# The order of the three products of a split-precision matmul: lower weights first instead of last

## The chip, the cores and the metric

One core of one Trainium2 chip runs the whole program, once per launch. The metric is device time in microseconds (us). The kernel before takes 658.43 us, the median of 3 runs that lie between 657.54 and 659.13.

## The reference, cut to what matters

The reference is a two-layer decoder trunk on 256 tokens of width 1024 in float32: a gated DeltaNet mixer, a squared-ReLU MLP (1024 to 4096 to 1024), a block-sparse attention mixer (with 256 tokens it is plain causal attention with a linear bias), a second MLP, and a final RMSNorm. What matters here are its dense products with weights:

```
proj = hn @ w_in                                  # DeltaNet: q, k, v, z
o.reshape(b, t, DN_DIM) @ w_out
jnp.square(jax.nn.relu(hn @ w_up)) @ w_down       # twice, once per layer
proj = hn @ w_in                                  # attention: q, k, v
o.transpose(0, 2, 1, 3).reshape(b, t, MB_DIM) @ w_out
```

The result must be close to float32 products, so the kernel splits both operands of each product into an upper part (rounded to the fast float32r format) and a lower part (what the rounding left over).

## The kernel before, in words

**Weights.** All weights come in one stream of 200 tiles ("units") of 128 x 1024 float32, 512 KB each. `prep` (lines 105 to 117) handles one: SyncE starts the DMA into `wf` (3 buffers), ScalarE casts it to the upper part `wh` (line 115, 5 buffers), and VectorE subtracts that from `wf` to get the lower part `wl` (line 116, 5 buffers). The first 8 units are handled in two halves of 512 columns. So of a tile `wh` is always there before `wl`. `unit` (line 121) hands out the next tile and first asks for the four after it (`LEAD = 4`), so that a tile's cast has to wait until TensorE has done with the tile five before it.

**Products.** `mm3` (lines 128 to 131) adds one weight block of 128 x 128 times one activation block of 128 x 256 into a PSUM accumulator, as three matmuls: upper weights by upper activations (line 129), upper weights by lower activations (line 130), lower weights by upper activations (line 131). The first argument after the output is the stationary operand, which is loaded into TensorE by a load of its own before each matmul (PEld in the profile); the second is streamed. The product of the two lower parts is left out. The first matmul of an accumulation carries `start`, the last one `stop`.

`mm3` is called from three places: `pair` (line 194: two columns of blocks over the 8 blocks of the input width, 48 matmuls from two units; used for q, k, v of both mixers and for the MLPs' first product), `project_out` (line 224: the mixers' output products) and `mlp` (line 267: the first layer's second MLP product, 4 outputs of 8 units each). Per unit this makes 8 calls, 24 matmuls. The products `natural` (lines 207 to 222; z and attention's v) and `mlp_last` (lines 322 to 345; the second layer's second MLP product) write their three matmuls with `mm` (line 133) and stream 512 columns of weights.

**Activations.** `Norm.feed` (line 164) makes upper and lower activations of a residual block: ScalarE the upper `xh` (line 167), VectorE the lower `xl` from it (line 168). `Norm.finish` (line 178) sums squares over partitions with small matmuls (`n_ps`) and spreads the scale with two more (`n_pb`, line 190); these stand between the matmuls of `pair` calls.

**Order.** Each engine executes its instructions in the order in which they stand in its queue. That order is made when the program is built: `ORDER` (line 47) and `ATT` (line 52) give the order in which the heads' steps are written, and the Tile framework's planner then takes, on its own costs, at each point the earliest-written instruction that it holds to be ready; it also sets the semaphore waits between engines. Where an instruction has more waits than it can carry, the rest go into EVENT_SEMAPHORE instructions ahead of it. So steps such as transposes and head matmuls stand between matmuls of one and the same `mm3`. VectorE (DVE) does everything in one queue: the `wl` subtractions, the lower activations, the evacuations of PSUM (line 258 in the MLP, lines 245 and 281 for the residual) and the mixers' elementwise steps.

Of the kernel before, what the change touches and what calls it, by code (L numbers as in the profile page):

```python
# [75 lines left out]
def trunk_kernel(ctx: ExitStack, tc: tile.TileContext, xT, wst, wba, par, con, selc, gfin, out):  # L76
    nc = tc.nc
# [48 lines left out]
        return ring[u]  # L126

    def mm3(o, wh, wl, xh, xl, start, stop):
        nc.tensor.matmul(o, wh, xh, start=start, stop=False, skip_group_check=True)  # L129
        nc.tensor.matmul(o, wh, xl, start=False, stop=False, skip_group_check=True)  # L130
        nc.tensor.matmul(o, wl, xh, start=False, stop=stop, skip_group_check=True)  # L131

    def mm(o, l, r, start=True, stop=True):
        nc.tensor.matmul(o, l, r, start=start, stop=stop, skip_group_check=True)  # L134
# [59 lines left out]
    def pair(nm, name):  # L194

        ps = bank("acc", [P, 2, T], f"ps_{name}")
        for c in range(2):
            wh, wl = unit()
            for k in range(4):
                kt = 4 * c + k  # L200
                for n in range(2):
                    s = slice((k * 2 + n) * P, (k * 2 + n + 1) * P)
                    mm3(ps[:, n, :], wh[:, s], wl[:, s], nm.xh[:, kt, :], nm.xl[:, kt, :],
                        kt == 0 and n == 0, kt == KT - 1)
        return ps
# [18 lines left out]
    def project_out(name, oh, ol, hin, nxt):  # L224

        pss = [bank("out" + "abcd"[i], [P, 2, T], f"ps_{name}_{i}") for i in range(4)]

        def piece(hd, n, w):
            s = slice(n * P, (n + 1) * P)
            mm3(pss[n // 2][:, n % 2, :], w[0][:, s], w[1][:, s], oh[:, hd, :], ol[:, hd, :],  # L230
                hd == 0 and n % 2 == 0, hd == H - 1)

        first = H - NLAST
        for hd in range(first):
            w = unit()
            for n in range(KT):
                piece(hd, n, w)
        w = [unit() for _ in range(first, H)]
        hout = act.tile([P, KT, T], F32, tag="h", name=f"h_{name}")
        for n in range(KT):  # L240
            for k in range(H - first):
                piece(first + k, n, w[k])
            if n % 2:
                i = n // 2
                nc.vector.tensor_add(hout[:, 2 * i:2 * i + 2, :], hin[:, 2 * i:2 * i + 2, :], pss[i])
                nxt.feed(hout, i)
        return hout
# [19 lines left out]
    def mlp(name, nm, hin, nxt):  # L267
        with tc.tile_pool(name=f"hid_{name}", bufs=1) as hp:
            hh, hl = mlp_up(hp, name, nm)
            hout = act.tile([P, KT, T], F32, tag="h", name=f"h_{name}")  # L270
            for i in range(KT // 2):
                ps = bank("acc", [P, 2, T], f"ps_dn_{name}_{i}")
                for c in range(8):
                    wh, wl = unit()
                    for k in range(4):
                        kt = 4 * c + k
                        for n in range(2):
                            s = slice((k * 2 + n) * P, (k * 2 + n + 1) * P)
                            mm3(ps[:, n, :], wh[:, s], wl[:, s], hh[:, kt, :], hl[:, kt, :],
                                kt == 0 and n == 0, kt == NFF - 1)  # L280
                nc.vector.tensor_add(hout[:, 2 * i:2 * i + 2, :], hin[:, 2 * i:2 * i + 2, :], ps)
                nxt.feed(hout, i)
        return hout
# [674 lines left out]
```

## Time and profile before

| | us |
|---|---|
| median of 3 runs | 658.43 |
| the profiled execution's own time | 658.23 |
| its span, first to last instruction | 656.4 |
| TensorE matmul busy | 643.4 (98%) |
| TensorE weight loads busy | 605.2 (92%) |
| VectorE busy | 454.6 (69%) |
| ScalarE busy | 345.6 (53%) |

What lies around the span is 658.23 - 656.4 = 1.8 us. In the profile PE is TensorE's matmuls, PEld its weight loads, DVE VectorE, ACT ScalarE, SP SyncE. A matmul row's duration is longer than the step to the next matmul, since matmuls overlap in the engine; where the pace matters, look at start times. By stage: DeltaNet from 10 to 181 us, the first MLP to 363, attention to 467, the second MLP to the end (its last product, by `mm`, from 560 on).

### The profile page before, as it was taken

What the parts mean: (1) busy time and instruction counts of PE and PEld (TensorE: products, weight loads), DVE (VectorE), ACT (ScalarE), POOL (GpSimd) and SP (SyncE); (2) the same over time, 40 slices, a digit from 0 to 9 for tenths busy, and PEclk for the clock granted to TensorE, in tenths of its full rate; (3) what the DMA queues carried; (4) which work ended last, traced back from release to release, by engine and by line L of the source; (5) the groups of instructions that cost most, each with busy time, mean ns of one, the idle gap of its engine ahead of it and who ended that gap; (6) DMA issues with size and microseconds to landing.
All of it is one profiled execution on the core that took longest, in us unless ns stands there. A gap on an engine that the chain in (4) does not pass through costs nothing.

```text
span 656.4 us, 13349 instructions
## 1 busy us (share of the span) xinstructions
PE 643.4 (98%) x5454; PEld 605.2 (92%) x5454; DVE 454.6 (69%) x841; ACT 345.6 (53%) x570; POOL 4.0 (1%) x10
## 2 busy tenths in 40 slices
PE   8999999999999999999999999999999999999995
PEld 6999878979999999999999999889999999888994
DVE  5899998997897666645554668775976666545443
ACT  7689782553575555534443444543655555434331
POOL 1000000000000000000000000000000000000000
PEclk9999999999999999999999999999999999999998
DMA  8754151342555555565555555555365555556531
GB/s 268 240 171 154 36 192 68 103 126 65 187 168 193 187 176 189 187 193 190 179 182 190 184 169 161 165 157 170 119 224 191 185 178 190 171 188 186 190 129 65
DMA packets 32029, 109.42 MB, mean 167 GB/s; under 512 B 3552, under 2 KB 3936, under 8 KB 31968
## 3 DMA queue, kind: packets, MB, share of 16 engines
q1 hardware_dynamic: 31248, 107.71, 49.9%
q8 instruction: 43, 0.70, 0.4%
q10 hardware_dynamic: 720, 0.86, 0.4%
q14 instruction: 18, 0.15, 0.1%
HBM read 107.51 MB, written 1.05 MB: 165 GB/s over the span
## 4 chain that ended last, share of the span: by engine, by line
PE 86%; DVE 6%; DMA 4%; ACT 3%; issue 1%; DVEq 0%; ACTq 0%
PE ps_last L134 12%; PE ps_up_m L130 9%; PE ps_up_m L131 9%; PE ps_up_m L129 9%; PE ps_dn_m L130 5%; PE ps_dn_m L129 5%; PE ps_dn_m L131 5%; PE ps_vn L134 3%; DMA wf<-in_w 3%; PE ps_z L134 3%; DVE wl L116 2%; PE ps_qk L130 2%; PE ps_qk L131 2%; PE ps_qk L129 2%; PE kk L134 2%; PE ps_last_e L134 1%
## 5 line engine op out<-in xcount | busy, mean ns | idle before, releaser
L116 DVE TENSOR_TENSOR wl<-wf,wh 128x1024 fp32r<-128x1024 f32 (+1 forms) x208 | 244.8, 1182 | 144.9 <-ACT wh L115 144.5
L115 ACT CAST wh<-wf 128x1024 fp32r<-128x1024 f32 (+1 forms) x208 | 210.7, 1017 | 244.3 <-PE ps_up_m L130 65.4
L130 PE MATMUL ps_up_m<-n_l,wh 128*128 128x256 f32 x512 | 143.9, 281 | 0.2 <-DVE n_l L168 0.2
L131 PE MATMUL ps_up_m<-n_h,wl 128*128 128x256 f32 x512 | 144.0, 281 | 0.0
L129 PE MATMUL ps_up_m<-n_h,wh 128*128 128x256 f32 x512 | 143.8, 281 | 0.0
L129 PEld LDWEIGHTS ps_up_m<-n_h,wh 128*128 128x128 f32 x512 | 98.0, 192 | 0.0
L130 PEld LDWEIGHTS ps_up_m<-n_l,wh 128*128 128x128 f32 x512 | 96.2, 188 | 0.3 <-DVE n_l L168 0.3
L131 PEld LDWEIGHTS ps_up_m<-n_h,wl 128*128 128x128 f32 x512 | 96.1, 188 | 0.0
L129 PE MATMUL ps_dn_m<-hh_m,wh 128*128 128x256 f32 x256 | 71.9, 281 | 0.0
L130 PE MATMUL ps_dn_m<-hl_m,wh 128*128 128x256 f32 x256 | 71.9, 281 | 0.0
L131 PE MATMUL ps_dn_m<-hh_m,wl 128*128 128x256 f32 x256 | 71.9, 281 | 0.0
L129 PEld LDWEIGHTS ps_dn_m<-hh_m,wh 128*128 128x128 f32 x256 | 49.2, 192 | 0.0
L130 PEld LDWEIGHTS ps_dn_m<-hl_m,wh 128*128 128x128 f32 x256 | 48.1, 188 | 0.0
L131 PEld LDWEIGHTS ps_dn_m<-hh_m,wl 128*128 128x128 f32 x256 | 48.1, 188 | 0.0
L134 PE MATMUL ps_last<-wh,hl_m 128*128 128x512 f32 (+1 forms) x128 | 46.9, 366 | 0.0
L134 PE MATMUL ps_last<-wl,hh_m 128*128 128x512 f32 (+1 forms) x128 | 46.8, 366 | 0.0
L134 PE MATMUL ps_last<-wh,hh_m 128*128 128x512 f32 (+1 forms) x128 | 46.7, 365 | 0.0
L129 PE MATMUL ps_kq<-n_h,wh 128*128 128x256 f32 x128 | 36.5, 285 | 0.0
L129 PE MATMUL ps_qk<-n_h,wh 128*128 128x256 f32 x128 | 36.3, 283 | 0.0
L131 PE MATMUL ps_kq<-n_h,wl 128*128 128x256 f32 x128 | 36.0, 281 | 0.0
L130 PE MATMUL ps_kq<-n_l,wh 128*128 128x256 f32 x128 | 35.9, 280 | 0.0
L130 PE MATMUL ps_qk<-n_l,wh 128*128 128x256 f32 x128 | 35.7, 279 | 0.0
(278 smaller groups left out, 1254.3 us busy)
## 6 DMA issues: line engine op xcount, KB each, us to landing
wf<-in_w SPq DMA_DIRECT2D x192, 512.0 KB, 3.5
wf<-in_w SPq DMA_DIRECT2D x16, 256.0 KB, 3.9
h<-in_x SPq DMA_DIRECT2D x4, 256.0 KB, 6.5
gf<-in_g SPq DMA_DIRECT2D x1, 512.0 KB, 3.8
out<-hg SPq DMA_DIRECT2D x2, 256.0 KB, 2.1
out<-hg ACTq DMA_DIRECT2D x2, 256.0 KB, 2.5
sel<-in_sel SPq DMA_DIRECT2D x1, 448.0 KB, 4.7
cn<-in_con SPq DMA_DIRECT2D x1, 276.0 KB, 5.1
```

The costliest lines, as they stand in the source:

```text
L115: nc.scalar.copy(wh[:, s], wf[:, s])
L116: nc.vector.tensor_sub(wl[:, s], wf[:, s], wh[:, s].bitcast(F32))
L129: nc.tensor.matmul(o, wh, xh, start=start, stop=False, skip_group_check=True)
L130: nc.tensor.matmul(o, wh, xl, start=False, stop=False, skip_group_check=True)
L131: nc.tensor.matmul(o, wl, xh, start=False, stop=stop, skip_group_check=True)
L134: nc.tensor.matmul(o, l, r, start=start, stop=stop, skip_group_check=True)
```

## The change: which product of the three comes first

Only the order of the three matmuls in `mm3` changes. `start` goes to lower weights by upper activations, `stop` to upper weights by lower activations. `natural`, `mlp_last` and everything else are as they were.

```diff
     def mm3(o, wh, wl, xh, xl, start, stop):
-        nc.tensor.matmul(o, wh, xh, start=start, stop=False, skip_group_check=True)
-        nc.tensor.matmul(o, wh, xl, start=False, stop=False, skip_group_check=True)
-        nc.tensor.matmul(o, wl, xh, start=False, stop=stop, skip_group_check=True)
+        nc.tensor.matmul(o, wl, xh, start=start, stop=False, skip_group_check=True)
+        nc.tensor.matmul(o, wh, xh, start=False, stop=False, skip_group_check=True)
+        nc.tensor.matmul(o, wh, xl, start=False, stop=stop, skip_group_check=True)
```

So after the change line 129 is lower weights by upper activations, line 130 upper by upper, line 131 upper weights by lower activations.

## Rows read from the trace of the kernel before

**Rows 1.** The page: span, busy time by engine, chain of waits by engine.
```profile
span 656.4 us, 13349 instructions
PE 643.4 (98%) x5454; PEld 605.2 (92%) x5454; DVE 454.6 (69%) x841; ACT 345.6 (53%) x570; POOL 4.0 (1%) x10
PE 86%; DVE 6%; DMA 4%; ACT 3%; issue 1%; DVEq 0%; ACTq 0%
```

**Rows 2.** Busy time by stretch: us, each engine's busy us (instructions), clock, DMA.
```profile
10.00:90.00 80.00, 78.39 (x589) 71.72 (x588) 75.96 (x207) 63.96 (x159) 1.05 (x2) 1.00 0.50 166
193.00:368.00 175.00, 175.00 (x1488) 175.00 (x1488) 104.87 (x110) 88.80 (x107) 0.00 (x0) 1.00 0.56 188
```

**Rows 3.** Line 129's matmuls: count, ns min/median/max, first to last start us.
```profile
L129 PE MATMUL ps_dn_m<-hh_m,wh x256: 281/281/281, 272.9 to 363.0; 128*128 128x256 f32 x128
...
L129 PE MATMUL ps_up_m<-n_h,wh x221: 281/281/281, 480.9 to 558.7; 128*128 128x256 f32 x111
...
L129 PE MATMUL ps_qk<-n_h,wh x45: 276/276/276, 378.0 to 392.9; 128*128 128x256 f32 x45
...
L129 PE MATMUL ps_a<-at_oh,wh x54: 276/276/276, 447.9 to 466.0; 128*128 128x256 f32 x54
...
L129 PE MATMUL ps_kq<-n_h,wh x128: 276/276/683, 10.1 to 64.8; 128*128 128x256 f32 x128
...
L129 PE MATMUL ps_g<-gd_oh,wh x64: 276/276/384, 150.8 to 180.6; 128*128 128x256 f32 x64
```

**Rows 4.** Timeline of PE around one break at 192 us: start, duration, operation.
```profile
191.90 0.28 PE L129 MATMUL ps_up_m<-n_h,wh 128*128 128x256 f32 x1
192.01 0.28 PE L130 MATMUL ps_up_m<-n_l,wh 128*128 128x256 f32 x1
192.13 0.60 PE L134 MATMUL n_pb<-cn,n_col 128*128 128x128 f32 x4
192.49 0.36 PE L131 MATMUL ps_up_m<-n_h,wl 128*128 128x256 f32 x1
192.69 0.28 PE L129 MATMUL ps_up_m<-n_h,wh 128*128 128x256 f32 x1
192.81 0.28 PE L130 MATMUL ps_up_m<-n_l,wh 128*128 128x256 f32 x1
```

**Rows 5.** Timeline of the first two weight tiles, 10.8 to 14.2 us.
```profile
10.80 0.69 DVE L116 TENSOR_TENSOR wl<-wf,wh 128x512 fp32r<-128x512 f32 x1 [0.18 <-ACT wh L115]
...
11.44 0.19 PEld L129 LDWEIGHTS ps_kq<-n_h,wh 128*128 128x128 f32 x1
...
11.66 0.19 PEld L131 LDWEIGHTS ps_kq<-n_h,wl 128*128 128x128 f32 x1
...
11.81 1.29 DVE L116 TENSOR_TENSOR wl<-wf,wh 128x512 fp32r<-128x512 f32 x2
...
14.16 0.19 PEld L129 LDWEIGHTS ps_kq<-n_h,wh 128*128 128x128 f32 x1
```

**Rows 6.** Who waited for whom: us in total, times, longest us.
```profile
PE kqt L507 <- DVE kq L500: 1.0, 1, 1.0
...
DVE wl L116 <- ACT wh L115: 144.5, 139, 3.3
ACT wh L115 <- PE ps_up_m L130: 65.4, 55, 2.1
```

**Rows 7.** Timeline of TensorE and DVE at the hand-over to the first MLP.
```profile
182.53 1.22 DVE L116 TENSOR_TENSOR wl<-wf,wh 128x1024 fp32r<-128x1024 f32 x1
...
183.67 0.39 PE L129 MATMUL ps_up_m<-n_h,wh 128*128 128x256 f32 x2
183.67 0.88 DVE L168 SCALAR_TENSOR_TENSOR n_l<-h_g,pm,n_h 128x256 fp32r<-128x256 f32 x2
...
184.21 0.38 PE L130 MATMUL ps_up_m<-n_l,wh 128*128 128x256 f32 x1 [0.15 <-DVE n_l L168]
```

**Rows 8.** Line 129's extra waits on TensorE's queue: count, ns, first and last start.
```profile
L129 PEldq EVENT_SEMAPHORE  x41: 51/51/51, 15.2 to 552.3; - x41
```

## The prediction

> **What bounds the kernel now.** I read the page first: TensorE's matmuls are busy 98% of the span, and the chain of waits that ended last lies to 86% on TensorE [rows 1]. So the question is what sets the pace of the matmul stream and where it is broken. Second the busy time by stretch: from 193 to 368 us matmuls and weight loads are busy 175.00 of 175.00 us while DVE works 104.87; from 10 to 90 us matmuls miss 1.6 of 80 us and DVE is nearly as full, 75.96 of 80 [rows 2]. There alone can a late weight tile matter.
>
> Third the starts of line 129, one per call of `mm3`, which give the pace. In the first MLP's second product 255 steps take 363.0 - 272.9 = 90.1 us: 0.3533 us per call, 117.8 ns per matmul. In the second MLP 220 steps take 77.8 us: 0.3536. But in attention 44 steps take 14.9 us and 53 steps 18.1 us, together 33.0 / 97 = 0.340 us, 113.4 ns per matmul [rows 3]. The same operation of the same shape has two paces, 3.9% apart, and the rows' durations (281 against 276 ns) tell which one a stretch has. A stretch keeps its pace; it changes only where other matmuls break in, as at 192.13, where `n_pb` stands between the upper and the lower product of one call: two starts before it are 0.11 apart, two behind it 0.12 [rows 4], and it then stays slow to 368 us. What chooses the pace I can't tell from the trace; it is the largest unknown.
>
> **The change part by part.** Nothing is added or removed: 24 matmuls and 24 loads per tile stay. Against the profiled execution's 658.23 us (span 656.4 and 1.8 around it), 0.2 below the median of 658.43.
>
> *The stream itself.* Write a call as (weights, activations): before (H,h)(H,l)(L,h), after (L,h)(H,h)(H,l). Calls follow one another without a break, so the stream of before, started one step later, is the stream of after: two uses of one upper tile side by side, then one lower; each load still overlaps the same kind of matmul. Only the step to the next block moves, from behind (L,h) to behind (H,l). A break then resumes at another member of the call. So I cost the pace at 0. Bounds: if both long slow stretches became fast, the first (175.0 us) would give 175.0 x (1 - 0.340/0.3533) = 6.6 us and the second (77.8 us) 3.0: -9.6. If the pieces whose median is 276 (128 + 64 + 45 + 54 = 291 calls in rows 3) became slow: 291 x 0.0133 = +3.9. I take 0, since it is the row with both members next to a break, `n_pb` in the middle of a call [rows 4], that the new order only renames.
>
> [...]
>
> *Lower weights asked for two matmuls earlier.* `wl` is ready after `wh`, and a call now begins with it. In the stream the cast waits for the release of an old tile (55 waits in the MLPs, rows 6), and then four tiles of 24 matmuls pass, 4 x 24 x 0.1178 = 11.3 us, before the new one is used; cast and subtraction need 2.3 of these (the subtraction is 1.22, rows 7). Two matmuls, 0.24 us, come off a margin of 9: nothing. At the start the margin is small. Tile 0's second half: DVE ends `wl` at 10.80 + 0.69 = 11.49, line 131 loads it at 11.66, and its first call begins at 11.44 [rows 5]. The load of 11.44 is now that of `wl`: with about 0.1 us from DVE's end to TensorE's start (the first of the two lower activations begun at 183.67 ends near 184.11, the matmul starts at 184.21, rows 7) it starts at 11.59, 0.15 late. Behind it wait only TensorE's own matmuls. Tile 1's first half ends near 12.46 and is due 12 matmuls after 11.44, at 12.80; its second half at 13.10 against 14.16 [rows 5]. No other is late. The 0.15 us is covered: at 32.85 TensorE waits 1.0 us for DVE's first head step anyway [rows 6], whose chain runs over DMA, ScalarE and DVE. Without that cover +0.15. I take 0.
>
> *Lower activations asked for later.* At 183.67 two upper products run ahead, then TensorE waits until 184.21 for `n_l` [rows 7]: 0.54 us for two matmuls of 0.113, so 0.32 idle. Now each of these two calls has two matmuls that don't need it; four run, to 183.67 + 4 x 0.1134 = 184.12, and 0.23 us of the wait is filled. Bounds 0 (the planner sets them otherwise) and -0.32. What is late next is the same DVE queue, where a `wl` subtraction of 1.22 us stands ahead of `n_l` [rows 7], so I take -0.2.
>
> *Upper weights released later.* `wh` is now read by the last matmul of a tile, one step of 0.118 us later; the cast starts that much later, and DVE, which waits 139 times for a cast [rows 6], holds what is queued behind its subtraction: residual adds, lower activations, evacuations. In the stream nobody waits for these (175.00 of 175.00). At the two output projections' hand-overs they lie ahead of the next matmuls: 0 to 2 x 0.12 = +0.24. At the one seen, the subtraction at 182.53 waits for no cast [rows 7], so 0.
>
> [...]
>
> *Waits on TensorE's queue.* Line 129 has 41 extra waits of 51 ns [rows 8]: it needs ScalarE's `wh` and, through DVE, a free accumulator. Now its weights come from DVE too, and `wh` is the wait of the next matmul, so many of the 41 may go: at most 41 x 0.051 = -2.1 us; as many new ones would be +2.1. Hidden by matmuls in flight in the full stretch [rows 2]: 0.
>
> Sum: 0 + 0 - 0.2 + 0 + 0 = -0.2: 658.0 for the profiled execution, 658.2 for the median.
>
> **The rivals.**
>
> *A: the fast pace is found (faster).* A break that resumes elsewhere leaves the long stretch from 193 us fast: 658.2 - 6.6 = 651.6; the stretch from 481 us alone 655.2; both 648.6. For it: the pace is chosen at a break, and nothing in the operation forbids 113.4 ns. Against it: both long stretches are slow, and the matmuls that break in stay what they are. Chance 0.17.
>
> *B: the extra waits counted.* If they were not hidden, 656.1. Against it: a steady pace over the many calls between 193 and 368 us. Chance 0.05.
>
> *C: the fast pace is lost (slower).* Place: the fast pieces of rows 3, in the two attention stretches and the DeltaNet's. It decides as soon as a break there resumes in the slow pace. Price: attention's 33.0 us alone x 3.9% = 1.3, 659.5; all 291 calls 3.9, 662.1; about half of them is 660.2, the value I give it. For it: these pieces are short, many breaks set them. Against it: breaks of the same kind follow. Chance 0.15.
>
> *D: DVE becomes the bound of the first 90 us.* If the load of `wl` waits at each of the first 8 tiles for its two matmuls, 8 x 0.23 = 1.8 and 660.0. It decides where DVE's 95% leaves a subtraction under 0.3 us of margin; rows 5 show this at one half tile only. Chance 0.06.
>
> *E: the change doesn't do what it says*, since the planner chooses among what it holds to be ready, and puts the products as before: 658.4, no change. Chance 0.03.
>
> **How the numbers follow.** The forecast, 658.2 us, has 0.54, and its own range is 657.0 to 659.5 (the small terms and the runs' spread of 1.6). About 0.2% or 1.3 us is what a measurement of this kernel can tell from no change. Same: forecast 0.54 and E 0.03, 0.57. Faster: A and B, 0.22. Slower: C and D, 0.21. The range goes down to A's first case, 651.5, and up past C's and D's values to 661.0; A with both stretches and C with all pieces are left out.
>
> **What would show it.** In the changed profile: line 129's starts in the second product of the first MLP still 0.353 apart and its rows at 281 ns; TensorE busy 98%; the wait for `n_l` near 184 us shorter; a wait of line 129 for `wl` near 11.4 us of some 0.1 us; fewer extra waits on line 129. The prediction is wrong if the long stretches show 276 ns (A), if attention shows 281 (C), or if TensorE waits for `wl` in many tiles before 90 us (D).

## The result: 1% slower, all of it lost in the first stage

The changed kernel takes 665.24 us (median of four, 664.24 to 668.64) against 658.32 of the kernel before: ratio 1.0102 [1.0074, 1.0129]. The forecast was 658.2 with a range of 651.5 to 661.0, so the time lies outside it, on the slower side. The profiled execution took 665.07, its span 663.3. (A ratio leaves out executions over 1.5% above their kernel's fastest; medians and lists below do not.)

The page of the changed kernel: span, busy time, chain of waits, and of the 40 slices TensorE's own and its clock.

```profile
span 663.3 us, 13324 instructions
...
PE 646.2 (97%) x5454; PEld 607.2 (92%) x5454; DVE 454.5 (69%) x841; ACT 348.0 (52%) x572; POOL 4.0 (1%) x10
...
PE   8999979999999999999999999999999999999995
...
PEclk9999997999999999999999999999999999999999
...
PE 85%; DVE 6%; ACT 4%; DMA 3%; issue 2%; ACTq 0%; DVEq 0%
```

Against [rows 1] nothing big has moved, but two slices stand out: TensorE is not full in the sixth, and its clock is down in the seventh, 100 to 116 us. The busy time by stretch (columns as in [rows 2]) confirms that the long stream is as before, 175.00 of 175.00, and shows the loss; first three stretches of the kernel before, then the same and the stream of the changed one:

```profile
90.00:100.00 10.00, 8.89 (x314) 7.75 (x313) 8.54 (x23) 8.64 (x15) 0.00 (x0) 1.00 0.56 180
100.00:110.00 10.00, 10.00 (x124) 8.45 (x122) 8.32 (x24) 2.69 (x5) 0.00 (x0) 1.00 0.28 100
110.00:126.00 16.00, 16.00 (x122) 14.57 (x121) 15.49 (x43) 5.98 (x11) 0.00 (x0) 1.00 0.22 67
```

```profile
90.00:100.00 10.00, 6.92 (x223) 5.80 (x223) 6.66 (x22) 9.53 (x14) 0.00 (x0) 1.00 0.50 157
100.00:110.00 10.00, 10.00 (x99) 9.05 (x99) 5.84 (x15) 4.21 (x7) 0.00 (x0) 0.66 0.19 56
110.00:126.00 16.00, 16.00 (x127) 13.58 (x128) 14.79 (x35) 4.06 (x5) 0.00 (x0) 1.00 0.31 101
...
199.00:374.00 175.00, 175.00 (x1489) 175.00 (x1488) 104.96 (x110) 88.88 (x107) 0.00 (x0) 1.00 0.57 188
```

In the timeline of TensorE the place is a run of 64 small matmuls (`pd` of the inversion, 32x32), which stops in the middle. Of the changed kernel:

```profile
90.68 0.69 PE L134 MATMUL pd<-xdt,y 32*32 32x32 f32 x56
91.89 0.26 PE L134 MATMUL pd<-xdt,y 32*32 32x32 f32 x8 [0.52 <-issue]
...
96.30 0.45 PE L134 MATMUL pd<-xdt,y 32*32 32x32 f32 x30
99.31 0.47 PE L134 MATMUL pd<-xdt,y 32*32 32x32 f32 x34 [2.56 <-issue]
...
100.99 0.41 PE L129 MATMUL ps_v<-n_h,wl 128*128 128x256 f32 x1
101.20 0.41 PE L130 MATMUL ps_v<-n_h,wh 128*128 128x256 f32 x1
```

"issue" says that nothing the profile shows was waited for: operands and accumulator were there for 30 of the 64 and no semaphore stands between them. Behind the 2.56 us the granted clock is at the lower of the two levels in the trace, 0.50 from 101 to 107 us, and a matmul's step is 0.21 us instead of 0.113. In the kernel before the same run takes 0.75 us in one piece:

```profile
96.55 0.75 PE L134 MATMUL pd<-xdt,y 32*32 32x32 f32 x64
```

By landmarks (same instruction, before and after): first z matmul 75.39 and 75.34; `py` (also small matmuls of the inversion) at 94.52 and 94.79; `pc` of the second half 153.47 and 160.34; `n_pb` 192.13 and 198.53; first down product 272.90 and 279.30; end 656.44 and 663.28. Up to 95 us nothing is lost, and from 160 us on the distance stays between 6.3 and 6.9.

The queues explain how a change of three lines gets there. SP and POOL have their order of before. But of ScalarE's 497 planned instructions 79 stand in another place, of DVE's 841 220, of TensorE's 4952 776: all of TensorE's lie in the first stage, and all but 3 of ScalarE's and 19 of DVE's, which lie in attention. The planner, for which a call now needs other tiles first, mixes the inversion, the heads' convolutions and the z products differently. So three things had changed at once: the products, the queues, and the pause.

### The profile page after: what moved, and what is told of

It reads as the page before. It is cut to its first block, busy times and chain, and to the rows that moved or that the text cites. A ratio compares the mean times of both kernels' runs of the same rounds, so it can differ in the third digit from the quotient of the medians.

```text
span 663.3 us, 13324 instructions
## 1 busy us (share of the span) xinstructions
PE 646.2 (97%) x5454; PEld 607.2 (92%) x5454; DVE 454.5 (69%) x841; ACT 348.0 (52%) x572; POOL 4.0 (1%) x10
## 4 chain that ended last, share of the span: by engine, by line
PE 85%; DVE 6%; ACT 4%; DMA 3%; issue 2%; ACTq 0%; DVEq 0%
PE ps_last L134 12%; PE ps_up_m L131 9%; PE ps_up_m L130 9%; PE ps_up_m L129 9%; PE ps_dn_m L130 5%; PE ps_dn_m L131 5%; PE ps_dn_m L129 5%; PE ps_vn L134 3%; PE ps_z L134 3%; DMA wf<-in_w 3%; PE ps_qk L130 2%; PE ps_qk L131 2%; PE ps_qk L129 2%; DVE wl L116 2%; PE ps_last_e L134 1%
## 5 line engine op out<-in xcount | busy, mean ns | idle before, releaser
L129 PEld LDWEIGHTS ps_up_m<-n_h,wl 128*128 128x128 f32 x512 | 98.1, 192 | 0.0
L130 PEld LDWEIGHTS ps_up_m<-n_h,wh 128*128 128x128 f32 x512 | 96.2, 188 | 0.0
L129 PE MATMUL ps_qk<-n_h,wl 128*128 128x256 f32 x128 | 36.4, 284 | 0.0
```

The costliest lines, as they stand in the source:

```text
L129: nc.tensor.matmul(o, wl, xh, start=start, stop=False, skip_group_check=True)
L130: nc.tensor.matmul(o, wh, xh, start=False, stop=False, skip_group_check=True)
```

## The experiments

**Products or queues.** Theory Q: the queues cost the 7 us; theory P: the products do. In e1 and e2 each engine's instructions are tied in a given order by order-only dependencies, written at the end of the kernel:

```
+    for x, y in zip(order, order[1:]):      # order: one engine's queue of the other kernel
+        tc.add_manual_dep(y, x.name, how, reason="plan")
```

> The products of the changed kernel, with every engine's queue held in the order of the kernel before (order-only dependencies, so no semaphore is added). Theory Q (the order of the queues that the planner chose around the inversion costs the 7 us): 658.3, within 0.5 of before, no matmul group that waits for issue over 1 us between 85 and 110 us. Theory P (the product order itself costs them, through the pace of the stream or later releases): 665.2, as the changed kernel.

Measured: 659.12, ratio 1.0001 [0.998, 1.0022]. With the queues of before the new products cost nothing. P falls.

> The reverse: the products of the kernel before, with every engine's queue in the order of the changed kernel. Theory Q: 665.2, with the pause of about 2.6 us in the run of 32x32 matmuls near 97 us and the clock at half behind it. Theory P: 658.3.

Measured: 661.53, ratio 1.0069 [1.0034, 1.0103]. The queues alone make it slower, but the ten executions are not alike: five from 660.15 to 660.88 at a mean clock of 0.996 to 0.998, three from 666.6 to 669.4 at 0.987 to 0.992, two between. The profiled one (660.46) has the 0.52 us pause and not the long one. So Q is right in kind, and the long pause is something that an execution has or has not.

In e3 and e4 the planner is free and part of the calls keeps the old order (`mm3` gets a flag from `pair`).

> The new product order only in the eight calls that project keys and queries (128 of the mm3 calls); all the rest as before. The planner is free and makes nearly the queues of the changed kernel (PE 117 places apart from it, 735 from before). Theory Q: 664 to 666, if the places that still differ do not touch the pause. Theory P, by the share of the calls: under 659.

Measured: 661.24, ratio 1.0053 [1.0029, 1.0078], three executions over 663.9. The new order in a tenth of the calls (128 of 1216) brings half of the loss, less than theory Q expected.

> The new product order everywhere but in the first stage's pair calls (keys, queries and values); the planner is free and leaves the queues almost as before (PE 30 places apart). Theory Q: 658.3, within 0.7. Theory P: 664 to 665, since nine of ten calls have the new order.

Measured: 659.21, ratio 1.0013 [0.9992, 1.0033]. The new order in the other 1024 calls brings nothing that can be told from none.

**The pause.** Which instruction does TensorE stop at? Counted in the trace, 1473 of its matmuls, loads and semaphore instructions stand before the first pause and 1729 before the second: 256 apart. And the DMA queue of instructions (q8) brings TensorE 16 KB at a time, 43 times: 43 x 256 = 11008, and TensorE has 10986 records in the trace. Its view from 91 to 96.7 us, of the kernel before:

```profile
q1 hardware_dynamic: 311, 1.13, 64.8%
q8 instruction: 1, 0.02, 1.1%
```

and of the changed kernel, which has no q8 in this stretch:

```profile
q1 hardware_dynamic: 214, 0.81, 50.7%
```

Its next block comes at 96.99, 0.24 us after TensorE stopped, lands at 97.96, and the matmuls go on at 99.31. Theory F: TensorE runs out of instructions, since 64 small matmuls are 128 instructions in 0.75 us, and a border between two blocks falls into such a run. In the profile of the kernel before TensorE's matmuls wait 0.2 us or more for "issue" nowhere; here they do twice, 0.52 and 2.56 us.

The test: put instructions that do nothing of use at the head of TensorE's queue. The order is held as in e1 and e2 (those lines are left out here; `Q` is 32), the operands stay, only the borders move against the runs.

```
     for _ in range(WARM):
         mm(pw[:, :T], wu[:, 0, :P], wu[:, 0])
+    for i in range(40):                     # 160 records; 48: 192, 44: 176
+        e = slice(i % 4 * Q, i % 4 * Q + Q)
+        mm(pw[e, :Q], wu[e, 0, :Q], wu[e, 0, :Q])
```

> The changed kernel once more, for the spread of its executions beside the others. Theory F (part of the loss is a pause of TensorE for its instructions, which an execution may or may not have): single times in two groups, about 660.5 and 664 to 669, most in the upper one. Theory D (the queues' order alone, the same in each execution): one group near 665.

Measured: 665.66, ratio 1.0085 [1.0051, 1.012]. Nine executions: 660.59, 660.62, 661.37, 663.53, and five from 665.66 to 668.17. The profiled one is the first of them: no pause at all, and a span of 658.7, that is 4.6 us less than with it:

```profile
90.71 0.75 PE L134 MATMUL pd<-xdt,y 32*32 32x32 f32 x64
...
96.06 0.76 PE L134 MATMUL pd<-xdt,y 32*32 32x32 f32 x64
```

D falls.

The first set of shifts used 40 to 56 matmuls of 128 rows by 16 columns. They held up the first product by 13 to 19 us, some 0.33 us each (0.22 at the full clock, 0.43 at the lower one, not the 0.32 at the half clock that e9's expectation names), so their times say little; the traces do.

> The changed kernel with its own queue order held, and 40 small warm-up matmuls (16 columns, 160 instruction records) put behind the sixth, before any data has come. Every later matmul keeps its place in the queue, but the borders between TensorE's blocks of 256 instructions fall 160 records earlier: outside the runs of 64 small matmuls at 89.5, 94.95 and 101.9 us instead of inside two of them (91.4 and 96.7 us). Theory F: no group that waits for issue over 0.3 us, the clock at 1.00 from 85 to 125 us, and 660.0 (659.0 to 661.0), what is left being the order itself. Theory D: 665 as before the shift, since the order is the same.

Measured: 673.57, no pause; from the first `py` to the end 569.2 us, where the changed kernel has 574.1 with its pause and 569.5 without.

> The same with 48 small matmuls (192 records): borders at 89.4, 94.82 and about 96.9 us, the last two 2.0 us apart with two runs of 64 small matmuls between them. Theory F: the pause is back, 1.5 to 2.5 us near 96.9 us, and 662 to 667. Theory D: 665, as with 160 records.

Measured: 679.92; a pause of 2.80 us in the last run, before record 1985 = 1729 + 256: a border again.

> The kernel before (old products, its own queue order held) with 56 small warm-up matmuls, 224 records: borders at 90.2 and 92.5 us, 2.3 us apart. Theory F: a pause of about 1.5 us near 92.5 us that the kernel before does not have, perhaps a second one behind it, and 660 to 666. Theory D: 658.3, since order and products are those of before.

Measured: 677.94; a miss, no pause. The block that was due at 111.51 was fetched at 109.03, as TensorE came to the border before it (109.22), had landed at 109.96 and was there in time. Two near borders were not enough here: the fetch came 2.5 us ahead of its border.

> The shift by 160 instruction records again, with 40 matmuls of 32x32 in place of 40 of 128x16, which took 0.32 us each at the half clock and held up the start by 13 us. They should take under 2.5 us in a stretch in which TensorE waits 1.8 us for data, so the start moves by at most 0.7 us. Changed kernel's products and queue order. Theory F (the pause for instructions): no pause in the runs of small matmuls, 660.6 (659.8 to 661.6), and no execution above 663, where the changed kernel has most of its own at 663 to 668. Theory D (the order alone): 665.5.

Measured: 661.01, ratio 1.0046 [1.0029, 1.0062], highest of six 662.99, no pause in the trace. The changed kernel's own queues, without the pause: 4.2 us less than the 665.24 with it.

> The same with 48 small matmuls, 192 records, where the run before had its pause of 2.8 us. Theory F: a pause of over 2 us in the last of the four runs of 64 small matmuls (about 97 us) in most executions, 664 to 668. Theory D: as with 160 records.

Measured: 665.56, ratio 1.0102 [1.0069, 1.0136], four executions from 662.45 to 668.46. Eight more small matmuls at the start, 80 us earlier, and the pause is back in the profiled one (667.44):

```profile
96.20 0.74 PE L181 MATMUL pd<-xdt,y 32*32 32x32 f32 x62
99.83 0.26 PE L181 MATMUL pd<-xdt,y 32*32 32x32 f32 x2 [2.89 <-issue]
```

> The kernel before (products and queue order), with 44 matmuls of 32x32 behind the warm-up, 176 records. The borders of 256 records that lie at 92.4 and 96.7 us in the kernel before come to 90.4, 94.5 and 97.1 us, the last two 2.5 us apart around two runs of 64 small matmuls. Theory F (the pause is a matter of where a border falls, whatever the products): a pause of 1 to 3 us at the last records of the second run, near 97.1 us, with the clock at half behind it in most executions, 661 to 666. Rival (only the changed order has the pause): 658.7, one group.

Measured: 667.53 (the ratio, 1.0077 [1.0027, 1.0127], counts seven of the ten); ten executions, two at 658.2 and 658.4, one at 662.4, seven from 665.8 to 668.8. The kernel before, with its own products and queues, gets the changed kernel's loss and more by a shift alone:

```profile
95.56 0.72 PE L181 MATMUL pd<-xdt,y 32*32 32x32 f32 x60
98.86 0.25 PE L181 MATMUL pd<-xdt,y 32*32 32x32 f32 x4 [2.58 <-issue]
```

No shift is needed either. Up to 193 us e12 (below) has the kernel before's own TensorE queue, and its profile shows two pauses, before records 2753 and 3009, which are 4 and 5 blocks of 256 behind 1729; from 145.3 to 152.2 us the clock is at its lower level, and a z step is 0.43 us instead of 0.23:

```profile
138.57 0.64 PE L181 MATMUL py<-xd,ua 32*32 32x32 f32 x51 [1.01 <-issue]
...
143.84 1.06 PE L181 MATMUL py<-xd,ua 32*32 32x32 f32 x31 [1.25 <-issue]
```

The profile of e4 has three shorter ones, of 0.42, 0.68 and 0.43 us, before records 1729, 2753 and 3009. So the pause is a risk that the kernel before runs too, and by the times it is frequent with the new queues: times of 663 us and more came in 10 of 13 executions of the changed kernel and in 3 of 86 of the kernel before.

F stands. What decides whether a block's fetch starts in time in a given execution stays open: in the changed kernel's profile no other DMA started from 90.1 to 93.1 us, so up to then it was not the queue of the weights that kept it, and with the same records it started at 92.1 us in the execution without the pause.

**The pace.** The largest unknown of the prediction was what chooses between 117.8 and 113.4 ns.

> Another question: the pace of the long streams. The kernel before (products and queue order), with four matmuls of one moving column more behind n_pb in both up projections (their result is used by nothing). In each profile so far the step is 113.5 ns behind n_ps (such columns) and 117.8 behind n_pb. Theory B (the last break sets the pace): 113.5 ns from 193 to 273 us at least and from 481 to 560 us; if it holds over the change of products at 273 us too, 658.4 - 6.6 - 3.0 + 0.6 for two more breaks = 649.4; if only the up streams gain, 3.1 + 3.0 less: 652.9. Theory R (the pace has another cause): 659.0, two more breaks of 0.3 us.

Measured: 660.47, ratio 1.0039 [1.0023, 1.0056]; both long stretches still at 117.8 behind the added matmuls. Of the first, in the columns of [rows 3]:

```profile
L176 PE MATMUL ps_dn_m<-hh_m,wh x256: 281/281/281, 273.0 to 363.1; 128*128 128x256 f32 x128
```

Taken by itself this speaks for R.

> For the pace: the kernel before (products and queue order) with a break of another kind ahead of each of the last 14 calls of both up projections, 14 kinds (1 to 8 matmuls of one moving column, of 64, 128 or 256 columns, 32x32 ones, and matmuls of the stream's own type), in the second projection in the reverse order; results of the breaks are used by nothing. Theory B (the kind of break sets the pace): the same kind gives the same step, 113.5 or 117.8 ns, in both projections, 14 of 14. Theory C (a matter of chance or of the moment): about 7 of 14 agree, and the same kernel's stretches change from one to the other. Time: 658.4 and some 28 breaks of 0.1 to 0.7 us, 664 to 670, up to 6 us less with the faster step.

Measured: 668.11, one execution. All 14 kinds agree between the two projections. Behind each short break (1 to 8 matmuls of one column, one of 2, 64 or 128, two of 128, 32x32 ones: 22 breaks) the step is 113; behind each break of 256 columns (6) it is 118. The last break of the first projection, one matmul of two columns, left the whole down product behind it at 113. Two kinds from its timeline (start, duration), first 32x32, then one matmul of the stream's own kind:

```profile
247.14 0.24 PE L181 MATMUL px_m<-n_acc 32*32 32x32 f32 x2
247.32 0.38 PE L176 MATMUL ps_up_m<-n_h,wh 128*128 128x256 f32 x1
...
247.90 0.28 PE L177 MATMUL ps_up_m<-n_l,wh 128*128 128x256 f32 x1
248.01 0.28 PE L178 MATMUL ps_up_m<-n_h,wl 128*128 128x256 f32 x1
248.12 0.28 PE L176 MATMUL ps_up_m<-n_h,wh 128*128 128x256 f32 x1
...
258.91 0.28 PE L181 MATMUL px_m<-n_h 128*128 128x256 f32 x1
259.03 0.28 PE L176 MATMUL ps_up_m<-n_h,wh 128*128 128x256 f32 x1
259.15 0.28 PE L177 MATMUL ps_up_m<-n_l,wh 128*128 128x256 f32 x1
259.26 0.28 PE L178 MATMUL ps_up_m<-n_h,wl 128*128 128x256 f32 x1
259.38 0.28 PE L176 MATMUL ps_up_m<-n_h,wh 128*128 128x256 f32 x1
```

The first goes 0.11 from start to start, the second 0.12, and so on to the next break.

> Where a break has to stand: the kernel before, in each of the last 14 pairs of both up projections first an extra matmul of 256 columns between two calls (which left the slower step 8 of 8 times), then, six calls on, a matmul of two columns ahead of the first, the second or the third product of a call, in turn. If place decides (n_pb in the middle of a call was followed by the slower step in the up projections each time): faster ahead of the first product, slower ahead of the second or third, the same in both projections. If only the kind decides: faster behind all 28. Time 660 to 664.

Measured: 660.28, one execution (the 8 in this expectation and the 25 in that of e14 are miscounted: 6 and 22). Place does not decide: behind all 28 two-column breaks, at each of the three places of a call, 113; behind all 28 extra matmuls of 256 columns 118. Why `n_pb`, two matmuls of 128 columns, and e11's one-column matmuls right behind it leave 118 all the same stays open.

The kernels' own breaks do not keep to the kind at all. Between two heads of attention the same break (`s`, then `ptp`) changed the step each time, in all 18 traces: a piece that followed one at 113 went at 118, and the other way round. In the kernel before the first piece is at 276 ns (`ps_qk` in [rows 3]); line 129 in the next three:

```profile
L129 PE MATMUL ps_qk<-n_h,wh x16: 281/281/363, 394.2 to 399.6; 128*128 128x256 f32 x16
...
L129 PE MATMUL ps_qk<-n_h,wh x16: 276/276/369, 400.8 to 406.0; 128*128 128x256 f32 x16
...
L129 PE MATMUL ps_qk<-n_h,wh x16: 281/281/476, 406.8 to 412.3; 128*128 128x256 f32 x16
```

`n_pb` was followed by 118 in the up projections, wherever enough matmuls stood behind it to tell, but ahead of attention by 113 in 11 traces and by 118 in 7. So what the added breaks do is shown; what chooses the step in general is not.

The use of it: one matmul of two columns, used by nothing, at the third pair of each up projection.

```
             for i in range(NFF // 2):
+                if i == 2:
+                    px = bank("norm", [P, 512], f"px_{name}")
+                    mm(px[:, :2], nm.acc[:, 0, :P], nm.acc[:, 1, :2])
                 ps = pair(nm, f"up_{name}_{i}")
```

> The kernel before (products and queue order) with one matmul of two moving columns ahead of the third call pair of each up projection, between two mm3 calls; its result is used by nothing. Theory B (a short break between two calls brings the faster step, 25 of 25 in the scan of breaks, and it lasts until the next break): 113.5 ns from 198 to 368 us and from 486 to 560 us, about 650.0 (658.5 - 6.3 - 2.9 + 0.3 = 649.6), at least 2 us less than before if only the up projections keep it. Rival (what the scan showed lasts for 48 matmuls but not over a change from the up to the down product): 652.9.

Measured: 649.26, ratio 0.9858 [0.983, 0.9885]; theory B. The step lasts over the change to the down product:

```profile
L176 PE MATMUL ps_dn_m<-hh_m,wh x256: 276/276/276, 269.9 to 356.6; 128*128 128x256 f32 x128
```

> The same two short breaks with the products of the changed kernel, in the queue order of the kernel before. If the order of the products has no part in the pace: 649.6 as well, within 1.0 of the run with the old products. If the edge that matters is between the two uses of one upper tile: the step stays at 117.8 ns and the time at 658.5 to 659.0.

Measured: 647.95, ratio 0.9836 [0.981, 0.9861]: faster than both kernels, and the new products neither hinder nor clearly help it (the two intervals overlap). Its line of the first product, count and durations as in [rows 3], has the long stretches at 276:

```profile
L176 PE MATMUL ps_up_m<-n_h,wl x512: 276/276/367, 180.3 to 550.1; 128*128 128x256 f32 x171
L176 PE MATMUL ps_dn_m<-hh_m,wl x256: 276/276/276, 269.5 to 356.2; 128*128 128x256 f32 x128
```

## Why the prediction was wrong, point by point

**The step that failed is the sum, by what it left out.** Every term asks what the new order does to its neighbours in queues that stay as they were. They did not stay: the planner made others for three engines. The prediction named the planner in one bound of the hand-over and in rival E, both times as a reason for no change; that it would keep the products and move what stands around them was no rival, and no term held a wait for instructions. Of the 6.9 us, 4.6 are the pause with the slow clock behind it (span 663.3 with, 658.7 without, the same kernel, one execution each), and 2.3 the queues themselves (658.7 against 656.4; the five lowest executions of e2 lie 1.8 to 2.6 above the median of the kernel before there, 658.31). Of these, 1.74 lie between the first z matmul and the first MLP. From the starts of TensorE's matmuls there, count and us, before and changed without the pause (e5):

```
                                          before        changed
mm3 to mm3                                302  37.84    305  39.02
z to z                                     75  18.78     64  16.81
one sort to another (mm3, z, small ...)   123  19.29    137  22.73
all steps of the stretch                      105.56       107.30
```

Fourteen more changes from one sort of matmul to another cost 3.44 us and the `mm3` steps 1.18 more; z on end takes 1.97 less and the rest 0.91. Part of this is only a z step that now leads to another sort and so stands in another row: all steps behind the 96 z matmuls together take 2.20 us more. Which move of the planner makes most of it was not told apart.

**The stream's pace, 0: right.** In the changed kernel line 129 (count, ns min/median/max, first to last start, as in [rows 3]) still has the slow pace:

```profile
L129 PE MATMUL ps_dn_m<-hh_m,wl x256: 281/281/281, 279.3 to 369.4; 128*128 128x256 f32 x128
```

255 steps in 90.1 us, 0.3533 each. `n_pb` stands in the middle of a call again, and behind it the steps are 0.12, as in [rows 4]:

```profile
198.42 0.28 PE L130 MATMUL ps_up_m<-n_h,wh 128*128 128x256 f32 x1
198.53 0.60 PE L134 MATMUL n_pb<-cn,n_col 128*128 128x128 f32 x4
198.90 0.36 PE L131 MATMUL ps_up_m<-n_l,wh 128*128 128x256 f32 x1
199.09 0.28 PE L129 MATMUL ps_up_m<-n_h,wl 128*128 128x256 f32 x1
199.21 0.28 PE L130 MATMUL ps_up_m<-n_h,wh 128*128 128x256 f32 x1
```

That the product order does not set the pace is what e14 and e15 show, and that a break can, e12 and e16. But the sentence that a stretch changes its pace only where other matmuls break in is wrong: at 184.21 [rows 7] TensorE did nothing but wait for `n_l`, and behind the wait the step is 0.118 where it had been 0.113. In the kernel before, 21 steps lie between these two:

```profile
184.43 0.28 PE L131 MATMUL ps_up_m<-n_h,wl 128*128 128x256 f32 x1
...
186.90 0.28 PE L131 MATMUL ps_up_m<-n_h,wl 128*128 128x256 f32 x1
```

Rival C happened in small: in attention some pieces changed from the one pace to the other, and from the first query product to the first of the last transposes (363.35 to 466.31, then 369.75 to 473.03) it costs 0.3 us. The reason against C, that breaks of the same kind follow, did not hold: the breaks are the same and the pace is not.

**Lower weights earlier, 0: right.** No load of line 129 waits for `wl`, not even the 0.1 us near 11.4 that was named as a sign; the z products start at 75.34 against 75.39. D, which priced such waits at 1.8 us, did not happen: in its first 90 us nothing was lost.

**Lower activations later, -0.2: wrong sign, small.** The wait at the hand-over [rows 7] grew from 0.15 to 0.26. Two matmuls ran ahead of it, as before, and not four, since in the planner's new queue the third product of a call stands right behind its second:

```profile
190.08 0.28 PE L130 MATMUL ps_up_m<-n_h,wh 128*128 128x256 f32 x1
...
190.62 0.39 PE L131 MATMUL ps_up_m<-n_l,wh 128*128 128x256 f32 x1 [0.26 <-DVE n_l L168]
```

**Upper weights released later, 0: right.** ScalarE waits for line 131 as it did for line 130 [rows 6]:

```profile
ACT wh L115 <- PE ps_up_m L131: 65.9, 55, 2.2
```

**Waits on TensorE's queue, 0: right.** 41 on line 129 [rows 8] became 38, with no effect to be seen.

Together these five are what e1 measures: 1.0001, between -1.3 and +1.4 us. The forecast for the product order was right and the forecast for the kernel was not. In the range, A's low end took the place that an unknown on the slower side should have had.

## What to carry to other kernels

Where a planner orders the queues, a change of a few lines can change several of them, here three of five: compare each engine's order before any row is argued from, and hold the order fixed when the edit itself is to be measured. Where runs of tiny matmuls stop, look at the borders between instruction blocks: here a wait for "issue" inside a run, with no semaphore (0.52 and 2.56 us), was their sign, and a shift of the code by 160 to 224 records tested it. And when one shape has two steps in one trace, scan what stands ahead of each: here two matmuls of two columns give 9 us, with the queues held.

## What the runs showed of the hardware

- TensorE stopped for 0.4 to 2.9 us, eleven times in seven traces, before records 1473, 1729, 1985, 2753 or 3009, which lie 256 or 768 apart. Each time the first instruction followed 1.2 to 1.5 us behind the landing of a 16 KB block of instructions; so a block can be late that landed before the stop (90.57 against 91.37 in the changed kernel's first pause). In the four long pauses the fetch began between 0.03 us before and 0.6 us after TensorE had stopped and took 0.9 to 1.4 us.
- After a pause of 2.56 us the granted clock is 0.66 over the stretch from 100 to 110 us and 0.50 from 101 to 107 us, with matmul steps of 0.213 us there. After the pauses of 1.01 and 1.25 us in e12 it fell too (z steps of 0.43 us); the three of 0.42 to 0.68 us in e4 left it at 1.00.
- 128x256 matmuls, each with its load, have two steady steps, 113.4 and 117.8 ns. An added break of up to 128 columns that stood alone led to the first in 50 of 50, one of 256 columns to the second in 34 of 34, and the step then lasted, in e12 and e14 over the 768 of the first MLP's down product. The kernels' own breaks of one kind led to either, and a wait without any other matmul changed the step as well.
- A float32 matmul of 128 rows by 16 columns, which is two records, took 0.22 us at the full clock and 0.43 at the lower one, to which it fell in e6 after 3 us of nothing else (0.7 in the first two of the 40 slices of its page). 32x32 ones on four groups of 32 partitions in turn cost almost nothing there (first product at 9.46 us with 40 of them, 8.95 and 9.11 without).
